# Row maxima of the next attention unit: spread over six pairs of key tiles instead of seven

## The chip, the core and the metric

The kernel runs on one core of a Trainium2 chip. The metric is the device time of one execution in microseconds (us); the figure for a kernel is the median of its runs. The engines are called as in the profile: PE (TensorE matrix products), PEld (TensorE loading its stationary operand), DVE (VectorE), ACT (ScalarE), POOL (GpSimd), SP (SyncE, which starts most DMAs here). Each engine works through its own queue in order.

## What is computed

One layer of a diffusion backbone on 2048 latent tokens and 256 context tokens, 1024 channels, in fp32: a modulated RMS norm, one wide input projection, two attention branches with gates, an output projection, a residual and a last norm. The branch the change touches is a full softmax attention of 8 heads, 2048 queries against 2304 keys (latent and context), key width 96, value width 64:

```python
sc = jnp.einsum('bqhd,bkhd->bhqk', qblk, k, preferred_element_type=jnp.float32) * scale
p = jax.nn.softmax(sc, axis=-1).astype(v.dtype)
return jnp.einsum('bhqk,bkhd->bqhd', p, v)
```

The other branch (neighbourhood attention on the 32 x 64 grid) runs at the same time in this kernel, as a side stream.

## The kernel before, in words

**Stages.** Projections first (up to about 1056 us of the profiled execution), then the attention stage (to about 2185 us), then the output projection. The change is in the attention stage.

**Units.** The full attention is cut into `nu = 32` units: unit `u` is head `u // 4` and a block of 512 queries `u % 4`. Within a unit the 2304 keys are 18 tiles of 128, taken in `NKP = 9` pairs (`kp` = 0 to 8). For each of the two tiles of a pair, PE makes scores `S` of 128 keys x 512 queries in three products (fp32 split in a high and a low part), and ACT takes the exponential into the pair's tile `P` (L1278). POOL adds the pairs' `P` into `za`, the softmax denominators (L1286, L1288, one instruction per pair). Every second pair, PE multiplies four tiles of `P` with the values into `oacc` (L1235).

**The row maximum.** The exponential needs the row's maximum beforehand. It is computed one unit ahead, by `max_tasks(u + 1)`: 20 parts, each one product `pm` of 128 queries x 512 keys (every fifth one 256 keys) on PE and one `reduce_max` on DVE (L825); then `fold`, a last small maximum on DVE (L828) followed on POOL by `spread` (L812), which lays the 512 maxima on diagonals in the tile `md`; and at last `row`, a product `pmf` of `md` with ones on PE and a copy by ACT into row 97 of the next unit's queries `qh` (L834). The 20 parts and the fold are a list of 21 tasks. `more` emits tasks of it three times per pair; `row` is emitted in the middle of the last pair (`kp == NKP - 1`), after the first tile's scores, and `zp` (the sum of the previous unit's denominators) with it.

**The side stream.** `feed` emits tasks of the neighbourhood attention at the same three places, by a count of its own: score products `ns`, products for its maxima `nm` and `nc` (evicted by DVE, L886 and L897), diagonals `nmd` on POOL (L812), their products `nf`, sums `nza` on POOL (L956, L937), values `no` on PE.

**What sets the order.** PE's order in this stage is the order in which the code emits its products (`keep_in_program_order`, L807-809). The queues of DVE, ACT, POOL and SP are put in order by a scheduler from the same code. All of `S`, `pm`, `pmf`, `zp`, `ns`, `nm`, `nc`, `nf` share five PSUM banks: `psm` gives them out from `psM` (three) and `psS` (two) in turn, and a bank is free again when DVE or ACT has read it. `P` has `PB = 8` tiles.

Of the kernel before, what the change touches and what calls it, by code (L numbers as in the profile page):

```python
# [64 lines left out]
def tile_hybrid_layer(ctx: ExitStack, tc: tile.TileContext, I: dict, out: bass.AP, dbg=None):  # L65
# [74 lines left out]
    def psm(name):  # L140
        if env["rot"] is not None:
            env["rot"] = (env["rot"] + 1) % 5
            if env["rot"] >= 3:
                return env["psS"].tile([P, W], F32, tag="S", name=name)
        return psM.tile([P, W], F32, tag="M", name=name)
# [627 lines left out]
    def load_qh(u):  # L773
        h, g = divmod(u, NB)
        qh = mq.tile([DK + 1, W], F32R, tag="qh", name=f"qh{u}", bufs=3)
        env["q"].dma_start(bc(qh[0:DK, :]), bc(qm[h][0, :, g * W:(g + 1) * W]))
        return qh

    def load_ql(u):
        h, g = divmod(u, NB)  # L780
        ql = mq.tile([DK, W], F32R, tag="ql", name=f"ql{u}")
        env["q"].dma_start(bc(ql), bc(qm[h][1, :, g * W:(g + 1) * W]))
        return ql

    def load_k(h):
        i = h % 2
        env["q"].dma_start(bc(Kh[i][0:NOPE, :]), bc(kmS[h][0]))
        env["q"].dma_start(bc(Kl[i][0:NOPE, :]), bc(kmS[h][1]))

    def load_v(h):  # L790
        vt = mv.tile([P, NKT, DV], F32, tag="V", name=f"V{h}")
        env["q"].dma_start(vt, vaS[:, h])
        return vt
# [12 lines left out]
    def mm(*args, **kw):  # L806
        ins = nc.tensor.matmul(*args, **kw)  # L807
        if pe["pin"]:
            tc.keep_in_program_order(ins)
# [5 lines left out]
    def max_tasks(u, qh):  # L815
        i = (u // NB) % 2
        m5 = mq.tile([P, 4, 5], F32, tag="m5", name=f"m5{u}")
        m1 = mq.tile([P, 4], F32, tag="m1", name=f"m1{u}")
        md = mq.tile([P, 4, P], F32R, tag="md", name=f"md{u}", bufs=1)

        def part(qt, ci):
            a, b = ci * W, min(NK, (ci + 1) * W)
            pm = psm(f"pm{u}_{qt}_{ci}")
            mm(pm[:, :b - a], qh[0:DK, qt * P:(qt + 1) * P], Kh[i][0:DK, a:b], start=True, stop=True)
            nc.vector.reduce_max(m5[:, qt, ci:ci + 1], pm[:, :b - a], axis=AX.X)  # L825

        def fold():
            nc.vector.tensor_reduce(m1, m5, axis=AX.X, op=ALU.max, negate=True)  # L828
            spread(md, m1)

        def row():
            pm = psm(f"pmf{u}")
            mm(pm, onesr, md.rearrange("p t f -> p (t f)"), start=True, stop=True)
            nc.scalar.activation(qh[DK:DK + 1, :], pm[DK:DK + 1, :], AF.Copy)  # L834
            for f in zdefer:
                f()
            zdefer.clear()

        return [lambda q=qt, c=ci: part(q, c) for qt in range(4) for ci in range(5)] + [fold], row
# [119 lines left out]
    def n_pv(d, pair, pts, last):  # L959
        h = d["h"]  # L960
        acc = d["acc"]
        vs = d["v"][:, :, (h % 2) * DV:(h % 2 + 1) * DV]
        lists = []
        for t, pt in zip(pair, pts):
            l = []
            if t[0] == "c":
                _, qc, ct = t
                half, bank = divmod(qc, 2)
                l.append((acc[half * DV:(half + 1) * DV, bank, :], vs[:, 16 + ct, :], pt, ct == 0))
            else:  # L970
                _, rb, cb = t
                (r0, r1), (c0, c1) = TROW[rb], CREG[cb]
                ncl = c1 - c0
                for sg in range(4):
                    a, b = max(r0, sg * 8), min(r1, sg * 8 + 8)
                    if a >= b:
                        continue
                    half, bank = divmod(sg, 2)
                    o_ = acc[half * DV:(half + 1) * DV, bank, :].rearrange("p (r c) -> p r c", c=GW)
                    l.append((o_[:, a - sg * 8:b - sg * 8, c0:c1], vs[:, rb * 4 + cb, :],  # L980
                              pt[:, (a - r0) * ncl:(b - r0) * ncl].rearrange("p (r c) -> p r c", c=ncl), False))
            lists.append(l)
        if len(lists[0]) == 3:
            lists[1] = lists[1][::-1]
        n = max(map(len, lists))
        for k in range(n):
            for l in lists:
                if k < len(l):
                    o_, v_, p_, st_ = l[k]
                    mm(o_, v_, p_, start=st_, stop=last and k == n - 1, skip_group_check=True)  # L990
# [171 lines left out]
    with tc.high_priority(offset=HOIST):  # L1162
        tasks, row = max_tasks(0, qhs[0])
# [7 lines left out]
    def feed(target):  # L1171
        while fed[0] < target:
            w_ = next(stream, None)
            if w_ is None:
                fed[0] = 1e9
                return
            fed[0] += w_
# [43 lines left out]
    NKP = NKT // 2  # L1221
# [7 lines left out]
    def pv(u, kp, pt, acc, za, vt):  # L1229
        late.append((kp, pt))  # L1230
        if kp % PVB == PVB - 1 or kp == NKP - 1:
            env["burst"] = True
            for k, p_ in late:
                for x in range(2):
                    mm(acc[x * DV:(x + 1) * DV, :], vt[:, 2 * k + x, :], p_[:, x, :],  # L1235
                                     start=(k == 0), stop=(k == NKP - 1), skip_group_check=True)
            late.clear()
        if kp < NKP - 1:
            return None
        oraw = mo.tile([DV, W], F32, tag="or", name=f"or{u}")  # L1240
        nc.scalar.activation(oraw, acc[DV:P, :], AF.Copy)
        nc.vector.tensor_tensor(oraw, acc[0:DV, :], oraw, op=ALU.add)
        return finish_tasks(u, za, oraw, pt)

    pe["pin"] = True
    for u in range(nu):
        h, g = divmod(u, NB)
        i = h % 2
        qh, ql = qhs[u], qls[u]
        vt = Vt  # L1250
        tasks, row = [], None
        if u + 2 < nu:
            qhs.append(load_qh(u + 2))
        if u + 1 < nu:
            tasks, row = max_tasks(u + 1, qhs[u + 1])
        if g == NB - 1 and h + 1 < H:
            Vt = load_v(h + 1)
        acc = psO.tile([P, W], F32, tag="O", name=f"oacc{u}")
        za = mo.tile([P, 2, W], F32, tag="za", name=f"za{u}")
        done = 0  # L1260
        prev = None
        for kp in range(NKP):
            pt = mp.tile([P, 2, W], F32, tag="P", name=f"P{u}_{kp}", bufs=PB)
            def more(frac):
                nonlocal done
                want = min(len(tasks), int(len(tasks) * (kp + frac) / (NKP - 2.0) + 1))
                while done < want:
                    tasks[done]()
                    done += 1

            for x in range(2):
                ks = slice((2 * kp + x) * P, (2 * kp + x + 1) * P)
                sp = psm(f"S{u}_{kp}_{x}")
                n = 0
                for a, b, e in ((Kh[i], qh, DK + 1), (Kh[i], ql, DK), (Kl[i], qh, DK)):
                    mm(sp, a[0:e, ks], b[0:e, :], start=(n == 0), stop=(n == 2))
                    n += 1
                nc.scalar.activation(pt[:, x, :], sp, AF.Exp)  # L1278
                more(0.33 * x)
                if x == 0 and kp == NKP - 1 and row is not None:  # L1280
                    row()
                if x == 0:
                    feed(total_weight * (step + 0.5 - LEAD) / (nsteps - TAIL - LEAD))
            ve = nc.vector if kp in ZDVE.get(nu - u, ()) else nc.gpsimd
            if kp == 1:
                ve.tensor_tensor(za, prev, pt, op=ALU.add)  # L1286
            elif 1 < kp < NKP - (u + 1 == nu):
                ve.tensor_tensor(za, za, pt, op=ALU.add)  # L1288
            prev = pt
            if kp == 1 and u + 1 < nu:  # L1290
                qls.append(load_ql(u + 1))
            if g == 0 and kp == 1 and h + 1 < H:
                load_k(h + 1)
            if pend is not None:
                ftasks = pv(*pend) or ftasks
                if env.pop("burst", False):
                    while held:
                        n_pv(*held.pop(0))
            pend = (u, kp, pt, acc, za, vt)
            if kp >= 2 and ftasks:  # L1300
                ftasks.pop(0)()
            more(0.66)
            step += 1
            feed(total_weight * (step - LEAD) / (nsteps - TAIL - LEAD))
# [239 lines left out]
```

## Time and profile before

| | us |
|---|---|
| median of 3 runs | 2565.34 (2562.31 to 2571.34) |
| profiled execution | 2569.03 |
| its span in the trace | 2567.2 |
| PE busy in the span | 2505.7 (98%) |
| DVE, POOL, ACT busy | 1102.7, 1092.2, 905.3 |

The profiled execution is one more run; its span is the stretch in which the trace shows instructions, 1.8 us less than its time. PE is the busiest engine by far, so the time is read from where PE waits and from the clock that it was granted; the other engines matter where PE waits for them.

### The profile page before, as it was taken

The page shows a single profiled execution, that of the slowest core. Times are in us where ns is not written, and L with a number is a line of the kernel's source. Part 1 is how long each engine was busy: PE and PEld are TensorE (multiplying, and loading weights), DVE is VectorE, ACT ScalarE, POOL GpSimd, SP SyncE. Part 2 cuts the span into 40 slices and gives each one's busy share as a digit, 9 for nine tenths or more (in the row PEclk, how much of TensorE's full clock was granted, in tenths as well). Part 3 has the DMA queues.
Part 4 walks back from the last instruction along what each step waited for, and adds up shares of the span by engine and source line. Part 5 has one row for each costly group of instructions (what it writes and reads, how often), then busy time and mean ns, then how long its engine had stood idle before and what let it go on. Part 6 is the DMA issues. An engine that isn't in the chain of part 4 may idle for free.

```text
span 2567.2 us, 34839 instructions
## 1 busy us (share of the span) xinstructions
PE 2505.7 (98%) x12796; PEld 1839.1 (72%) x12796; DVE 1102.7 (43%) x2285; ACT 905.3 (35%) x1774; POOL 1092.2 (43%) x861
## 2 busy tenths in 40 slices
PE   7999999999999999999999999999999999999998
PEld 4878888877789888656555656665656664888998
DVE  4653222222311211355455635554646446455654
ACT  3664432222222122234444434444444444212221
POOL 1312111111310000368787868777887885132220
PEclk9999999999999999999999989999999999999999
DMA  7535765456553465712324141514140334765542
GB/s 263 191 92 164 257 222 185 140 167 191 178 159 109 122 214 194 184 48 68 80 51 107 46 101 36 121 39 109 39 110 26 81 106 144 246 190 161 181 148 70
DMA packets 182979, 342.86 MB, mean 134 GB/s; under 512 B 25130, under 2 KB 95950, under 8 KB 175438
## 3 DMA queue, kind: packets, MB, share of 16 engines
q1 hardware_dynamic: 168872, 299.01, 38.9%
q0 software_dynamic: 13504, 41.35, 5.6%
q8 instruction: 100, 1.64, 0.3%
q14 instruction: 71, 0.58, 0.1%
q10 hardware_dynamic: 432, 0.28, 0.0%
HBM read 214.42 MB, written 126.13 MB: 133 GB/s over the span
## 4 chain that ended last, share of the span: by engine, by line
PE 88%; DVE 3%; DMA 3%; POOL 2%; issue 2%; ACT 1%; SPq 1%; POOLq 0%; ACTq 0%; DVEq 0%
PE accm L135 25%; PE S L807 15%; PE oacc L807 10%; PE pm L807 6%; PE f L135 5%; PE ya L135 4%; PE vacc L135 4%; PE nacc L226 3%; PE no L807 3%; PE accf L135 2%; PE accx L135 1%; PE qa_False L135 1%; PE pstl L185 1%; PE nm L807 1%; POOL za L1288 1%
## 5 line engine op out<-in xcount | busy, mean ns | idle before, releaser
L825 DVE TENSOR_REDUCE m<-pm 128x1 f32<-128x512 f32 (+1 forms) x640 | 387.6, 632 | 420.0 <-PE pm L807 414.3
L1288 POOL TENSOR_TENSOR za<-za,P 128x1024 f32<-128x1024 f32 x217 | 516.1, 2378 | 114.2 <-ACT P L1278 110.7
L1278 ACT ACTIVATE P<-S 128x512 f32<-128x512 f32 x576 | 342.9, 597 | 481.3 <-PE S L807 465.9
L135 PE MATMUL accm<-hh,whi 128*128 128x512 f32 x928 | 366.7, 395 | 0.0
L135 PE MATMUL accm<-hh,wlo 128*128 128x512 f32 x928 | 366.4, 395 | 0.0
L135 PE MATMUL accm<-hl,whi 128*128 128x512 f32 x928 | 366.3, 395 | 0.0
L807 PE MATMUL oacc<-P,V 128*64 128x512 f32 x1152 | 292.0, 624 | 0.0
L807 PE MATMUL S<-qh,Kh 97*128 97x512 f32 x576 | 240.4, 417 | 7.9 <-DVE m L825 4.3
L807 PE MATMUL S<-ql,Kh 96*128 96x512 f32 x576 | 230.7, 400 | 0.0
L807 PE MATMUL S<-qh,Kl 96*128 96x512 f32 x576 | 229.3, 398 | 0.0
L807 PE MATMUL pm<-Kh,qh 96*128 96x512 f32 (+1 forms) x640 | 222.6, 395 | 4.5 <-DVE m L825 3.3
L135 PEld LDWEIGHTS accm<-hh,whi 128*128 128x128 f32 x928 | 174.1, 188 | 42.8 <-issue 0.8
L135 PEld LDWEIGHTS accm<-hh,wlo 128*128 128x128 f32 x928 | 174.1, 188 | 42.5
L135 PEld LDWEIGHTS accm<-hl,whi 128*128 128x128 f32 x928 | 174.1, 188 | 41.6
L807 PEld LDWEIGHTS pm<-Kh,qh 96*128 96x128 f32 x640 | 121.1, 189 | 106.7 <-issue 62.5
L135 PE MATMUL ya<-u,woh 128*128 128x256 f32 x1024 | 185.0, 283 | 2.0 <-DVE t L1346 2.0
L807 PEld LDWEIGHTS oacc<-P,V 128*64 128x64 f32 x1152 | 70.4, 139 | 137.6 <-issue 137.3
L135 PE MATMUL f<-wfh,y 128*128 128x512 f32 (+1 forms) x528 | 162.2, 387 | 6.2 <-DMA wfh<-wfS 4.0
L135 PEld LDWEIGHTS ya<-u,woh 128*128 128x128 f32 x1024 | 160.1, 192 | 3.2 <-DVE t L1346 2.4
L807 PEld LDWEIGHTS S<-qh,Kh 97*128 97x128 f32 x576 | 109.9, 191 | 54.0 <-issue 12.4
L135 PE MATMUL ya<-u,wol 128*128 128x256 f32 x512 | 144.8, 283 | 0.0
L356 ACT ACTIVATE g<-accm 128x512 f32<-128x512 f32 x88 | 52.2, 593 | 248.8 <-PE accm L135 202.6
(1928 smaller groups left out, 4253.2 us busy)
## 6 DMA issues: line engine op xcount, KB each, us to landing
rawc<-in_wch SPq DMA_DIRECT2D x30, 512.0 KB
KA<-kB SPq DMA_DIRECT2D x16, 576.0 KB
xl<-in_xb SPq DMA_DIRECT2D x32, 256.0 KB
wm<-in_wmodb SPq DMA_DIRECT2D x8, 1024.0 KB
kmS<-sk POOLq DMA_DIRECT2D x32, 256.0 KB, 3.8
qR<-q SPq DMA_DIRECT2D x16, 512.0 KB
qm<-sq POOLq DMA_DIRECT2D x32, 256.0 KB, 4.1
woS<-ps SPq DMA_DIRECT2D x16, 512.0 KB
```

Of the source, the lines that this page charges most:

```text
L135: nc.tensor.matmul(acc, a, b, start=(i == 0), stop=(i == n - 1))
L185: nc.tensor.matmul(pst[32 * j:32 * j + 32, :w], ones[:, 0:32], sq[:, :w], start=(kt < 4), stop=(kt >= 4))
L226: nc.tensor.matmul(acc[:, :n], a[:, k, sl], b[:, k, :n], start=(k == 0 and q == 0), stop=(k == KT - 1 and q == 2))
L356: nc.scalar.activation(s1, acc, AF.Sigmoid)
L807: ins = nc.tensor.matmul(*args, **kw)
L825: nc.vector.reduce_max(m5[:, qt, ci:ci + 1], pm[:, :b - a], axis=AX.X)
L1278: nc.scalar.activation(pt[:, x, :], sp, AF.Exp)
L1288: ve.tensor_tensor(za, za, pt, op=ALU.add)
```

## The change

One number: the divisor that spreads the 21 tasks over the unit.

```diff
             def more(frac):
                 nonlocal done
-                want = min(len(tasks), int(len(tasks) * (kp + frac) / (NKP - 2.0) + 1))
+                want = min(len(tasks), int(len(tasks) * (kp + frac) / (NKP - 3.0) + 1))
                 while done < want:
                     tasks[done]()
                     done += 1
```

Tasks emitted at the three places of a pair (after the first tile's scores, after the second's, at the pair's end), counted out from that line:

| pair | before | now |
|---|---|---|
| 0 | 1, 0, 1 | 1, 1, 1 |
| 1 | 2, 0, 1 | 1, 1, 1 |
| 2 | 2, 0, 1 | 2, 1, 1 |
| 3 | 2, 0, 1 | 1, 1, 1 |
| 4 | 2, 0, 1 | 2, 1, 1 |
| 5 | 2, 0, 1 | 1, 1, 1 |
| 6 | 2, 0, 1 | 1 (the fold) |
| 7 | 1 (the fold) | none |
| 8 | none | none |

`row` stays in pair 8, so two pairs lie between fold and row where there was one. No instruction is added or removed on any engine.

On PE, in pair 5 of unit 11 (`pm12_a_b` is the product of query block a and key block b for unit 12; `S11_5_x` the scores of tile x; `ns2` a score of the side stream). Before:

```order
L807 MATMUL S11_5_0_12004<-qh11_11198,Kh0_8342 128x512
L807 MATMUL S11_5_0_12004<-ql11_11555,Kh0_8342 128x512
L807 MATMUL S11_5_0_12004<-qh11_11198,Kl0_8344 128x512
L807 MATMUL pm12_2_4_12009<-Kh1_8343,qh12_11493 128x256
L807 MATMUL pm12_3_0_12012<-Kh1_8343,qh12_11493 128x512
L807 MATMUL ns2_('w', 1, 3)_12015<-QQ_8341,KA_8339 128x360
L807 MATMUL ns2_('w', 1, 3)_12015<-QLt_8338,KBt_8340 128x360
L807 MATMUL S11_5_1_12022<-qh11_11198,Kh0_8342 128x512
L807 MATMUL S11_5_1_12022<-ql11_11555,Kh0_8342 128x512
L807 MATMUL S11_5_1_12022<-qh11_11198,Kl0_8344 128x512
L807 MATMUL pm12_3_1_12028<-Kh1_8343,qh12_11493 128x512
```

Now:

```order
L807 MATMUL S11_5_0_12013<-qh11_11198,Kh0_8342 128x512
L807 MATMUL S11_5_0_12013<-ql11_11558,Kh0_8342 128x512
L807 MATMUL S11_5_0_12013<-qh11_11198,Kl0_8344 128x512
L807 MATMUL pm12_3_2_12018<-Kh1_8343,qh12_11493 128x512
L807 MATMUL ns2_('w', 1, 3)_12021<-QQ_8341,KA_8339 128x360
L807 MATMUL ns2_('w', 1, 3)_12021<-QLt_8338,KBt_8340 128x360
L807 MATMUL S11_5_1_12028<-qh11_11198,Kh0_8342 128x512
L807 MATMUL S11_5_1_12028<-ql11_11558,Kh0_8342 128x512
L807 MATMUL S11_5_1_12028<-qh11_11198,Kl0_8344 128x512
L807 MATMUL pm12_3_3_12033<-Kh1_8343,qh12_11493 128x512
L807 MATMUL pm12_3_4_12037<-Kh1_8343,qh12_11493 128x256
```

Two products, then one, have become one, then two, and the last product of the unit (3_4) stands here instead of in pair 6.

On POOL, around the spread `md12` in the same unit (`P11_k` is pair k's tile). Before:

```order
L1288 TENSOR_TENSOR za11_11816<-za11_11816,P11_5_12003 128x1024
L956 TENSOR_TENSOR nza2_11145<-nza2_11145,np2_('w', 1, 3)_12016 128x15x24
L956 TENSOR_TENSOR nza2_11145<-nza2_11145,np2_('w', 2, 3)_12032 128x15x24
L1288 TENSOR_TENSOR za11_11816<-za11_11816,P11_6_12038 128x1024
L812 TENSOR_TENSOR md12_11812<-ident_63,m112_11811 128x512
```

Now:

```order
L1288 TENSOR_TENSOR za11_11816<-za11_11816,P11_5_12012 128x1024
L956 TENSOR_TENSOR nza2_11145<-nza2_11145,np2_('w', 1, 3)_12022 128x15x24
L812 TENSOR_TENSOR md12_11812<-ident_63,m112_11811 128x512
L956 TENSOR_TENSOR nza2_11145<-nza2_11145,np2_('w', 2, 3)_12041 128x15x24
L1288 TENSOR_TENSOR za11_11816<-za11_11816,P11_6_12047 128x1024
```

The spread has moved ahead of pair 6's addition; so it has in 30 of the 31 units that have one, and in the last of them (unit 30) it stays behind it.

On DVE, in unit 12, around the first window maxima of the side stream's next head (`nm4_0`, `nm4_1`; `nc4_0` its context maximum; L886 ISA with 128x1 reads the result out). Before:

```order
L825 TENSOR_REDUCE m513_12134<-pm13_3_1_12330 128x1
L897 TENSOR_REDUCE nmx4_12265<-nc4_0_12333 128x2
L825 TENSOR_REDUCE m513_12134<-pm13_3_2_12343 128x1
L825 TENSOR_REDUCE m513_12134<-pm13_3_3_12346 128x1
L886 ISA njk4_0_12288,nmx4_12265<-nm4_0_12286,bn4_11902 128x264
L886 ISA nmx4_12265 128x1
L886 ISA njk4_1_12305,nmx4_12265<-nm4_1_12303,bn4_11902 128x352
```

Now:

```order
L825 TENSOR_REDUCE m513_12134<-pm13_3_4_12339 128x1
L828 TENSOR_REDUCE m113_12135<-m513_12134 128x4
L897 TENSOR_REDUCE nmx4_12271<-nc4_0_12342 128x2
L886 ISA njk4_0_12294,nmx4_12271<-nm4_0_12292,bn4_11905 128x264
L886 ISA nmx4_12271 128x1
L886 ISA njk4_1_12314,nmx4_12271<-nm4_1_12312,bn4_11905 128x352
```

The two window maxima still stand behind row maxima whose products PE makes later; they now follow the context maximum of pair 5 directly instead of two row maxima of pair 6.

## Rows read from the trace of the kernel before

**Rows 1.** The page: busy time by engine; the chain that ended last, by engine.
```profile
PE 2505.7 (98%) x12796; PEld 1839.1 (72%) x12796; DVE 1102.7 (43%) x2285; ACT 905.3 (35%) x1774; POOL 1092.2 (43%) x861
PE 88%; DVE 3%; DMA 3%; POOL 2%; issue 2%; ACT 1%; SPq 1%; POOLq 0%; ACTq 0%; DVEq 0%
```

**Rows 2.** Windows: start:end, length, PE PEld DVE ACT POOL busy (instructions), PEclk, DMA.
```profile
1080.00:2185.00 1105.00, 1077.44 (x5207) 654.85 (x5207) 593.26 (x1187) 486.62 (x877) 848.24 (x506) 0.98 0.31 78
```

**Rows 3.** Waits, 1080 to 2185: who waited for whom, total, times, longest.
```profile
PEld pmf L807 <- POOL md L812: 16.8, 13, 3.5
PE pmf L807 <- POOL md L812: 11.8, 6, 3.0
```

**Rows 4.** Timeline of PE, four of the six waits for the spread: start, length, instruction.
```profile
1338.49 0.51 PE L807 MATMUL pmf<-md,onesr 128*128 128x512 f32 x1 [2.09 <-POOL md L812]
...
1482.44 0.49 PE L807 MATMUL pmf<-md,onesr 128*128 128x512 f32 x1 [2.23 <-POOL md L812]
...
1989.73 0.50 PE L807 MATMUL pmf<-md,onesr 128*128 128x512 f32 x1 [2.21 <-POOL md L812]
...
2157.71 0.79 PE L807 MATMUL pmf<-md,onesr 128*128 128x512 f32 x1 [3.05 <-POOL md L812]
```

**Rows 5.** Timeline of POOL ahead of the wait at 1482.44 (unit 11).
```profile
1474.76 2.38 POOL L1288 TENSOR_TENSOR za<-za,P 128x1024 f32<-128x1024 f32 x1
1477.08 0.96 POOL L956 TENSOR_TENSOR nza<-nza,np_('w', 1, 3)_12016 128x360 f32<-128x360 f32 x1
1478.12 0.95 POOL L956 TENSOR_TENSOR nza<-nza,np_('w', 2, 3)_12032 128x360 f32<-128x360 f32 x1
1479.03 2.36 POOL L1288 TENSOR_TENSOR za<-za,P 128x1024 f32<-128x1024 f32 x1
1481.35 1.04 POOL L812 TENSOR_TENSOR md<-ident,m 128x512 fp32r<-128x512 f32 x1
```

**Rows 6.** Timeline of DVE in pairs 5 to 7 of unit 11.
```profile
1472.91 0.69 DVE L825 TENSOR_REDUCE m<-pm 128x1 f32<-128x512 f32 x1
1473.52 0.52 DVE L953 TENSOR_TENSOR np_('w', 2, 3)_12032<-ns_('w', 2, 3)_12031,bt 128x360 f32<-128x360 f32 x1
...
1478.15 0.42 DVE L825 TENSOR_REDUCE m<-pm 128x1 f32<-128x256 f32 x1 [2.69 <-PE pm L807]
1478.61 0.17 DVE L828 TENSOR_REDUCE m<-m 128x4 f32<-128x20 f32 x1
```

**Rows 7.** Windows of 8 us behind the waits at 1338.49 and 1989.73.
```profile
1338.50:1346.50 8.00, 8.00 (x42) 4.32 (x43) 1.33 (x3) 2.39 (x6) 8.00 (x5) 0.79 0.52 130
...
1989.70:1997.70 8.00, 7.97 (x57) 5.01 (x59) 1.66 (x3) 2.87 (x6) 7.84 (x5) 1.00 0.15 49
```

**Rows 8.** DVE's fold and POOL's spread of unit 30, from the timelines.
```profile
2156.37 0.17 DVE L828 TENSOR_REDUCE m<-m 128x4 f32<-128x20 f32 x1
2156.62 1.04 POOL L812 TENSOR_TENSOR md<-ident,m 128x512 fp32r<-128x512 f32 x1 [1.35 <-DVE m L828]
```

**Rows 9.** Unit 12: PE's product nm4_0 and a wait, DVE's maximum of nm4_0, a window.
```profile
1504.45 0.29 PE L807 MATMUL nm<-NKm,NQs 112*128 112x264 f32 x1
...
1513.46 0.80 PE L807 MATMUL nc<-NKm,NQs 112*128 112x256 f32 x2 [0.78 <-DVE m L825]
1517.72 0.42 DVE L886 CUSTOM_DVE_ANT_1 njk<-nm,bn 128x264 f32<-128x264 f32 x1
1509.00:1526.00 17.00, 14.45 (x36) 7.54 (x37) 5.61 (x14) 3.68 (x7) 6.52 (x4) 0.60 0.00 0
```

**Rows 10.** Groups by form, 1080 to 2185: DVE's full row maxima, busy, mean ns, idle before.
```profile
L825 DVE TENSOR_REDUCE m<-pm 128x1 f32<-128x512 f32 x485 | 322.8, 686 | 295.7 <-PE pm L807 291.1
```

**Rows 11.** Tile pm, 1080 to 2185: who waited for these products and maxima, us, times.
```profile
  PEld S L807: 7.9, 12
...
  PE S L807: 3.0, 5
  PE pm L807: 2.6, 2
```

## The prediction

> **What bounds the kernel now.** I read the page first: PE is busy for 98% of the span and holds 88% of the chain that ended last [rows 1], so nothing but PE's waits and PE's clock can give time back. Then the window over the attention stage: of 1105 us PE is busy for 1077, its mean granted clock is 0.98, and DVE and POOL work 54% and 77% of the stage [rows 2]. So 28 us are idle there, and a clock of 0.98 means another 22 us or so lost at the half rate. The list of waits then says who holds PE: the largest single cause is the product `pmf`, which waits for POOL's spread `md`, 11.8 us in six waits [rows 3]. The rest is many small waits for PSUM banks. The change acts on exactly these two kinds, and only in this stage.
>
> Four of the six waits are shown [rows 4], 9.6 us together; the two left out, in units 18 and 29, share the other 2.2 us. Five of the six have one cause, and one another. In unit 11 the maxima are folded by 1478.8 [rows 6], yet the spread starts at 1481.35 [rows 5]: POOL is behind, and the addition of pair 6 (2.36 us) stands ahead of the spread in its queue. PE is ready for `pmf` 2.23 us before it gets it [rows 4], at 1480.2. In unit 30 it is the other way round: POOL sat idle for 1.35 us until DVE folded at 2156.37 [rows 8]; there DVE is late.
>
> **The change part by part.** No instruction is added or taken away; what changes is places in queues.
>
> *1. The spread moves ahead of pair 6's addition on POOL.* For unit 11 I lay the new order on the old times: pair 5's addition and the first `nza` sum end at 1478.04, the spread runs to 1479.1 (1.04 us) [rows 5], and PE asks for it at 1480.2: 1.1 us to spare. The fold must be there by 1478.04. The last product now stands where the product of DVE's row at 1472.91 stood, with one short product and one side-stream row behind it; adding 0.42, 0.52 and 0.17 to the end of that row (1473.60) gives about 1474.7 [rows 6], 3 us early. At the other four waits of this kind the spread passes at least one addition of 2.36 us too, and the longest of the five waits is 2.23 us [rows 4, 5]; so I take all five as gone: 11.8 - 3.05 = 8.8 us, with 8.8 us as the best and half of it as the worst (if the fold or another piece of POOL's backlog is late in its place). What the spread passes is late by its 1.04 us: the addition of pair 6 and, in some units, an `nza` sum or an `nmd`. Behind these additions stand the reuse of a `P` tile (eight tiles, so eight pairs of cover), the unit's last sum, which PE asks for in the next unit's pair 8, and the side stream's `nf`. If that cover were gone, 1.04 us per unit would show, at most where POOL is behind, five times: 5 us; I take nothing.
>
> *2. The clock behind these waits.* Behind the wait at 1338.49 the clock reads 0.79 over 8 us, which is 8 x 0.21 = 1.7 us lost, and so it does, three times in all, behind the waits of units 11 and 18; behind the one at 1989.73 it reads 1.00 [rows 7]. The clock is either 1.2 or 2.4 GHz, and it fell after idle stretches of about 2 us in three cases of four. Waits gone, I take 3 x 1.7 = 5.1 us back; between 0 and 5.1 us.
>
> *3. Unit 30.* The spread stays behind pair 6's addition, and the fold is set by DVE, which is busy with the output stage's first inputs there. The products come a pair earlier but DVE's queue ahead of the fold holds nearly the same work. I take 0, between 0 and -3.05 us.
>
> *4. More row maxima per pair.* Pairs 0, 2 and 4 get one product more, pair 6 loses three. In pairs 2 and 4 the extra one stands right ahead of the four value tiles, when PE needs no new bank for a while; but the odd pairs now end on two products and the next pair begins with two, so four maxima (4 x 0.69 us [rows 10]) fall due around one group of scores, where it was three. That happens about twice in a unit, in 31 units: 62 places. The nearest rows are the waits for DVE's maxima as they are: 3.0 + 2.6 us on PE in seven waits, and 7.9 us on PEld, which mostly hide behind running products [rows 11]. Taken in proportion to the density (20 products in 6 pairs instead of 6 1/3) hardly 1 us is added; if all the PEld waits came to the surface, 7.9 us. I take +2 us, near the low end, because DVE has 295.7 us of idle time ahead of these maxima [rows 10]; the range is 0 to +7.9 us, and rival B is beyond it.
>
> *5. The banks held by the side stream.* In unit 12 PE makes `nm4_0` at 1504.45, but DVE reads it only at 1517.72, since its queue has row maxima of later products ahead [rows 9], as the order on DVE in the section on the change shows. Two of five banks are held meanwhile, PE stumbles in short waits, and the clock over 1509 to 1526 reads 0.60: 17 x 0.40 = 6.8 us lost, and 17 - 14.45 = 2.55 us idle [rows 9]. Now DVE reads it after the context maximum of pair 5, so between `nm4_1` and its release PE makes seven groups instead of ten. Three tenths of 6.8 + 2.55 = 9.4 us is -2.8 us; in unit 16 the next head's first maximum is held somewhat longer than before, for which I set +0.8 us. I take -2 us; the bounds are -9.4 us (the whole episode goes) and +9.4 us (a second one like it).
>
> The sum: -8.8 - 5.1 + 0 + 2 - 2 = **-13.9 us**. Against the profiled execution's own 2569.0 us that is 2555.1 us; the median of the runs is 3.7 us lower than that execution, so the forecast for the median is 2565.3 - 13.9 = 2551.4 us, **2551 us**. The work in other stages is the same.
>
> **The rivals.**
>
> *A. The waits go, but not the time: about 2559 us.* Half of the waits stay in another form (the spread stands in time, but now waits for a fold that DVE delays, or PE meets POOL's backlog later at `nf`), so -4.4 us instead of -8.8 and half of the clock, -2.6; with parts 4 and 5 as taken, -7 us. For it speaks that POOL is 77% busy in the stage and its backlog is work, not order [rows 2]; against it that the fold is 3 us early in unit 11 by its rows [rows 6], and that nothing asks POOL for a result within the next pairs.
>
> *B. Denser maxima make PE stumble: slower, about 2575 us.* In unit 12, with banks short, a wait of 0.78 us for DVE and shorter ones like it stand in the long stretch at 0.60, worth 9.4 us [rows 9]. If four maxima around one group of scores are too many for five banks, such stretches come elsewhere too. The point from which it decides: without part 4's +2 and part 5's -2 the gain is 13.9 us, so two such episodes (18.8 us) bring the kernel back to about 2570 us, and slower by over 0.3% (7.7 us) needs 21.6 us, two and a bit; I price it at 2.5, 2565.3 - 13.9 + 23.5 = 2575 us. Speaking against it: in 28 or so of the other units with three maxima there is no such stretch, and the extra product mostly stands ahead of the value tiles. The Trainium skill (TensorE: Matmul & The Clock Gate, section "A second HAM failure mode: psum-queue depth-cycling") describes this: a kernel that cycles through PSUM banks leaves PE idle for so short and so often that the clock swings between its two levels; by that rule the change, which asks more of the banks, would end as B. The trace agrees with it at this one stretch and shows no other like it in the stage.
>
> *C. The unit 12 episode goes altogether: about 2544 us.* Then part 5 is -9.4 instead of -2: 2565.3 - 21.3 = 2544 us. Seven groups on three banks may be few enough; the order alone can't tell.
>
> *D. The change doesn't do what it says.* The order shows the spread moved in 30 of 31 units; only in unit 30 is it not, which is part 3. No chance of its own.
>
> **How the numbers follow.** Forecast (2546 to 2557 us) 0.45; C (2539 to 2546) 0.16; A (2557 to 2566) 0.26; B (2566 to 2585) 0.13. The range that holds the time 8 times in 10 leaves a tenth at each end: 2541 to 2569 us. A measurement of this kernel can tell about 0.3%, 7.7 us, from no change: faster means below 2557.6, slower above 2573.0. Faster: forecast and C, and a little of A, 0.61. Slower: most of B, 0.10. Within 0.3%: 0.29.
>
> **What would show it right or wrong.** Part 1 is right if the list of waits has `pmf` behind `md` at about 3 us, one wait, in unit 30; wrong if several of 1 to 2 us are left. Part 2: the windows behind pair 8 of units 7, 11 and 18 read 1.00. Part 3: the wait of unit 30 stays between 2 and 3 us. Part 4: who waited for the maxima: PE's share stays under 8 us; over 15 us it was mis-sized. Part 5: the stretch of unit 12 reads a mean clock over 0.60 and less idle time. B shows as a stretch of a clock of 0.60 or less in any other unit. The prediction as a whole is wrong if PE's idle time in the stage falls by 9 us and the span doesn't, or if the clock of the stage falls under 0.98.

## The result: 29 us faster, twice the forecast

The changed kernel takes 2535.8 us, the median of four runs (2531.7 to 2539.3), beside 2564.6 us for the kernel before (2562.3 to 2571.3): a ratio of 0.988, 95% interval 0.986 to 0.989. Measured once more beside other kernels it was 2535.6 us, a ratio of 0.988 (0.987 to 0.990). The forecast was 2551 us with a range from 2541 us on; the sign was right, the size was half of what came, and the time lies 5 us below the range. Its profiled execution took 2537.2 us, its span 2535.4 us.

The page answers [rows 1] with busy time by engine and the chain by engine:

```profile
PE 2489.2 (98%) x12796; PEld 1833.4 (72%) x12796; DVE 1105.9 (44%) x2285; ACT 903.1 (36%) x1774; POOL 1093.5 (43%) x861
PE 89%; DMA 3%; DVE 3%; SPq 1%; ACT 1%; issue 1%; POOL 1%; POOLq 0%; DVEq 0%; ACTq 0%
```

PE has the same 12796 instructions and is busy for 16.5 us less. It did no less work: the granted clock, averaged over the execution, has gone from 0.987 to 0.995, so fewer of its instructions ran at the half clock. The window over the same stretch of the attention stage answers [rows 2] (columns as there):

```profile
1080.00:2185.00 1105.00, 1088.84 (x5423) 675.36 (x5422) 604.82 (x1197) 486.33 (x885) 848.79 (x510) 0.99 0.33 85
```

216 PE instructions more fit into the same 1105 us, PE is idle for 16 us instead of 28, and the clock has gone from 0.98 to 0.99. Of the waits behind the spread, [rows 3], this is what is left:

```profile
PEld pmf L807 <- POOL md L812: 3.6, 1, 3.6
PE pmf L807 <- POOL md L812: 3.2, 1, 3.2
```

One wait, the one of unit 30. To see where the rest went, I cut the stage into its 32 units: a unit's time runs from the start of its first product `S<-qh,Kh` to the start of the next unit's first (each unit has 18; the last unit runs to the end of the stage's last product `oacc`). Changed kernel less kernel before, in the two profiled executions:

| units | part of the prediction | forecast, us | measured, us |
|---|---|---|---|
| 7, 11, 18, 25, 29 | 1 and 2 | -13.9 | -3.9 -4.1 -3.9 -2.4 -0.5 = -14.8 |
| 30, 31 | 3 | 0 | +0.4 +0.6 = +0.9 |
| 12, 16 | 5 | -2.8 +0.8 = -2 | -6.8 +0.3 = -6.5 |
| the other 22, without unit 0 | 4 | +2 | -1.7 |
| 0 | none | none | -5.8 |
| outside the stage | none | 0 | -4.0 |

They add up to -31.8 us, the difference of the two spans (2567.2 and 2535.4). The last row is no effect of the change: what lies outside the stage was 1.9 to 6.6 us shorter than in that one execution of the kernel before in every later profile, in kernels that change a single unit too. Without it the stage is 27.8 us shorter, near the 28.8 us between the medians.

**Parts 1 and 2, as forecast.** POOL in unit 11, which answers [rows 5], and PE's `pmf` there:

```profile
1461.95 2.38 POOL L1288 TENSOR_TENSOR za<-za,P 128x1024 f32<-128x1024 f32 x1
1464.29 0.96 POOL L956 TENSOR_TENSOR nza<-nza,np_('w', 1, 3)_12022 128x360 f32<-128x360 f32 x1
1465.21 1.04 POOL L812 TENSOR_TENSOR md<-ident,m 128x512 fp32r<-128x512 f32 x1
...
1467.13 2.39 POOL L1288 TENSOR_TENSOR za<-za,P 128x1024 f32<-128x1024 f32 x1
```
```profile
1467.48 0.40 PE L807 MATMUL pmf<-md,onesr 128*128 128x512 f32 x1
```

The spread ends at 1466.25, PE asks at 1467.48: 1.2 us to spare, where 1.1 us had been worked out from [rows 5]. The windows behind the `pmf` of units 7, 11 and 18, which answer [rows 7], read a full clock:

```profile
1328.80:1336.80 8.00, 8.00 (x52) 4.51 (x53) 2.87 (x5) 4.56 (x10) 8.00 (x7) 1.00 0.52 131
1467.50:1475.50 8.00, 8.00 (x57) 4.34 (x55) 1.38 (x2) 4.24 (x8) 7.76 (x4) 1.00 0.89 194
1714.60:1722.60 8.00, 8.00 (x57) 4.47 (x55) 1.30 (x2) 3.48 (x7) 7.76 (x6) 1.00 0.82 191
```

**Unit 0, which the prediction does not name.** In the kernel before, PE's waits in the first microseconds of the stage were these, with the two row maxima of DVE that released the first two:

```profile
1061.65 0.49 PE L807 MATMUL pm<-Kh,qh 96*128 96x512 f32 x1 [0.78 <-DVE m L825]
1062.93 0.50 PE L807 MATMUL S<-qh,Kh 97*128 97x512 f32 x1 [0.78 <-DVE m L825]
1064.53 0.79 PE L807 MATMUL S<-qh,Kh 97*128 97x512 f32 x1 [0.52 <-DVE m L825]
```
```profile
1060.90 0.69 DVE L825 TENSOR_REDUCE m<-pm 128x1 f32<-128x512 f32 x1 [0.25 <-PE pm L807]
1062.18 0.69 DVE L825 TENSOR_REDUCE m<-pm 128x1 f32<-128x512 f32 x1 [0.59 <-PE pm L807]
```

DVE reads at 1060.90 the product that PE has just made (it started at 1060.47), and is through at 1061.59; at 1061.65 PE starts the next one. It then waits for DVE to read that one (until 1062.87) before it starts a group of scores. So each waits for the bank of its immediate predecessor, although the stage has five banks. The whole unit, as a window of the kernel before and one of the changed kernel:

```profile
1057.80:1093.10 35.30, 33.08 (x127) 19.59 (x128) 19.25 (x45) 12.61 (x20) 21.19 (x12) 0.90 0.91 216
```
```profile
1055.60:1085.10 29.50, 29.36 (x127) 18.48 (x128) 19.19 (x45) 12.57 (x20) 21.09 (x12) 1.00 1.04 241
```

The same 127 PE instructions: 2.1 us less idle time, and 0.10 x 35.3 = 3.5 us less lost to the clock.

**Unit 12.** Windows over the unit, before and after, and the three waits that are left:

```profile
1489.10:1531.60 42.50, 39.56 (x151) 21.55 (x150) 18.50 (x36) 16.02 (x27) 23.28 (x13) 0.84 0.40 98
```
```profile
1472.50:1508.10 35.60, 33.55 (x151) 19.57 (x150) 18.77 (x36) 15.90 (x27) 26.43 (x15) 1.00 0.53 130
```
```profile
1493.08 0.50 PE L807 MATMUL pm<-Kh,qh 96*128 96x512 f32 x1 [0.75 <-ACT P L1278]
1495.77 0.39 PE L807 MATMUL pm<-Kh,qh 96*128 96x256 f32 x1 [0.79 <-DVE m L825]
1496.67 0.51 PE L807 MATMUL nc<-NKm,NQs 112*128 112x256 f32 x2 [0.52 <-DVE m L825]
```

Still 2.06 us of waits, where there were 2.94 us of idle time before; but the 0.16 x 42.5 = 6.8 us that the half clock took are gone.

**What the built program says.** Which of the five banks a tile gets is fixed when the kernel is built: the code asks the two pools for tiles in turn (three from the one, two from the other), but within a pool a tile gets whichever bank the scheduler takes for free at that point, and that can be the one just used. The banks in pairs 0 to 2 of unit 0, in PE's order:

```
before: S0_0_0 0  pm1_0_0 2  S0_0_1 1  pm1_0_1 3  S0_1_0 4  pm1_0_2 2  pm1_0_3 2  S0_1_1 2  pm1_0_4 3  S0_2_0 3
now:    S0_0_0 0  pm1_0_0 2  S0_0_1 1  pm1_0_1 3  pm1_0_2 4  S0_1_0 2  pm1_0_3 0  S0_1_1 1  pm1_0_4 3  pm1_1_0 4  S0_2_0 2
```

Bank 2 three times running and bank 3 twice: these are the three waits. Over the stage a tile gets the bank of the tile made just before it 8 times in the kernel before (units 0, 9, 12, 23) and 7 times in the changed one (units 9, 12, 16, 27). Unit 12 has three of the 8 and four of the 7, so the number of repeats alone does not tell what a unit loses. So the change moved the spread and, by the way, dealt out the banks anew: units 0 and 23 are clear of it, 16 and 27 now have one each.

### The profile page after: what moved, and what is told of

Its sections match the earlier page's. It is cut to its first block, busy times and chain, and to the rows that moved or that the text cites. A ratio compares the mean times of both kernels' runs of the same rounds, so it can differ in the third digit from the quotient of the medians.

```text
span 2535.4 us, 34849 instructions
## 1 busy us (share of the span) xinstructions
PE 2489.2 (98%) x12796; PEld 1833.4 (72%) x12796; DVE 1105.9 (44%) x2285; ACT 903.1 (36%) x1774; POOL 1093.5 (43%) x861
## 4 chain that ended last, share of the span: by engine, by line
PE 89%; DMA 3%; DVE 3%; SPq 1%; ACT 1%; issue 1%; POOL 1%; POOLq 0%; DVEq 0%; ACTq 0%
PE accm L135 26%; PE S L807 15%; PE oacc L807 10%; PE pm L807 6%; PE f L135 5%; PE ya L135 4%; PE vacc L135 4%; PE nacc L226 3%; PE no L807 3%; PE accf L135 2%; PE accx L135 1%; PE nm L807 1%; DMA rz<-rzS 1%; PE pstl L185 1%; PE qa_False L135 1%
## 5 line engine op out<-in xcount | busy, mean ns | idle before, releaser
L807 PE MATMUL oacc<-P,V 128*64 128x512 f32 x1152 | 286.7, 614 | 0.0
```

## The experiments

The theory after this result: the gain has three causes, (a) the spread's place in POOL's queue, (b) the bank given twice running in unit 0, (c) the side stream's held banks in unit 12, which leave three banks for everything else. Rivals: that the earlier products do it by themselves, that the stretches of half clock in units 0 and 12 come and go by chance, or that unit 12's stumbling follows from unit 11's wait. "Unit" times are differences to the kernel before, as in the table above, each from one profiled execution.

**One group of units at a time.** First the change in unit 0 alone:

```diff
-                want = min(len(tasks), int(len(tasks) * (kp + frac) / (NKP - 2.0) + 1))
+                want = min(len(tasks), int(len(tasks) * (kp + frac) / (NKP - (3.0 if u == 0 else 2.0)) + 1))
```

> The denser spread only in unit 0; the other units as in the kernel before. Theory (order in the unit): in the profile of before, unit 0 has three PE waits for banks (0.78, 0.78, 0.52 us) around 1063 us and then 6.8 us at the half clock, and in the changed kernel neither; if the order of the products in unit 0 did that, unit 0 takes about 29.5 us here instead of 35.3 us, and the kernel gains 5 to 6 us (ratio 0.998). Rival (chance of the execution): the half clock there comes and goes by itself; unit 0 may then read 35 us here, and the times are the same as before within 2 us. Rival (my prediction's sum): nothing in unit 0, 0 us.

2563.7 us beside 2567.3, ratio 0.998 (0.997 to 0.999). Unit 0 is 5.7 us shorter and at full clock; unit 12, built as before, reads 42.5 us and 0.84 again:

```profile
1055.90:1085.50 29.60, 29.41 (x127) 18.49 (x128) 19.20 (x45) 12.62 (x20) 21.14 (x12) 1.00 1.04 240
1483.30:1525.80 42.50, 39.56 (x152) 21.57 (x151) 18.50 (x36) 16.01 (x27) 23.29 (x13) 0.84 0.40 99
```

The gain of unit 0 belongs to what the edit does in that unit. Then the five units with a wait behind POOL, by the same line with `u in (7, 11, 18, 25, 29)`:

> The denser spread only in units 7, 11, 18, 25 and 29, where the product pmf waited for the spread behind POOL's addition. Theory: the pmf waits of these units go, and with them 14 to 15 us (2550 us, ratio 0.994); unit 12 keeps its long stretch at the half clock (42 us) and unit 0 its 35 us. Rival (unit 12's stretch is a follow-up of unit 11's wait 27 us earlier): unit 12 falls to about 36 us here too, and the kernel gains 21 us. Rival (the waits are worth only their own 8.8 us and the clock comes back as low elsewhere): 9 us.

2550.2 us beside 2567.3, ratio 0.993 (0.992 to 0.994). One `pmf` wait is left (unit 30), the five units are 14.8 us shorter, just as in the changed kernel. Unit 12 is 1.1 us shorter only: it does not follow from unit 11. Unit 0, unaltered, had a shorter stretch of half clock here (-1.4 us). Then unit 12 alone, `u == 12`:

> The denser spread only in unit 12. Theory (the banks held by nm4_0 and nm4_1 are free sooner by the order in this unit): unit 12 takes 35 to 36 us instead of 42.5, no half clock of 13.65 us there, and the kernel gains 7 us (ratio 0.997). Rival (follow-up of unit 11's wait, which stays here): unit 12 stays at 42 us, 0 us. Rival (my prediction's part 5): about three tenths, 2.8 us, with a shorter stretch at the half clock left.

2562.1 us beside 2567.3, ratio 0.998 (0.997 to 0.999); unit 12 is 5.2 us shorter, while unit 11 keeps its wait:

```profile
1487.20:1524.40 37.20, 35.16 (x150) 20.06 (x150) 18.78 (x36) 15.90 (x27) 23.18 (x13) 0.95 0.42 105
```

A clock of 0.95, 1.9 us lost, where the first profile of the changed kernel had 1.00. Which of the two comes differs from execution to execution: the second profile of the changed kernel, below, has 0.95 too.

**The fold left where it was.** Products as in the changed kernel, but the fold emitted in pair 7:

```diff
-                want = min(len(tasks), int(len(tasks) * (kp + frac) / (NKP - 2.0) + 1))
+                want = min(len(tasks) - (kp < NKP - 2), int(len(tasks) * (kp + frac) / (NKP - 3.0) + 1))
```

> The products spread over six pairs in all units as in the changed kernel, but the fold left in pair 7. Theory (the waits for the spread come from the place of the fold and the spread in POOL's queue): the pmf waits of units 7, 11, 18, 25, 29 are back, about 9 us, and the half clock behind some of them, so the gain against before is only what units 0 and 12 give, 12 to 13 us, and some 15 us are lost against the changed kernel (about 2551 us). Rival (the products' earlier end alone does it, since POOL then has less backlog): the pmf waits stay away and the time is that of the changed kernel, 2536 us.

My expectation fell: 2538.6 us beside 2567.3, ratio 0.989 (0.988 to 0.990), the changed kernel's time, and the five units 14.8 us shorter. But the rival's reason is not shown by it either, for POOL's row in unit 11 reads

```profile
1460.40 0.97 POOL L956 TENSOR_TENSOR nza<-nza,np_('w', 1, 3)_12022 128x360 f32<-128x360 f32 x1
1461.33 1.04 POOL L812 TENSOR_TENSOR md<-ident,m 128x512 fp32r<-128x512 f32 x1
1462.33 0.97 POOL L956 TENSOR_TENSOR nza<-nza,np_('w', 2, 3)_12041 128x360 f32<-128x360 f32 x1
```

Though the code emits the fold in pair 7, the scheduler puts the spread ahead of pair 6's addition in 28 of the 30 units (not in units 0 and 26, where PE does not wait for it either). So it is the earlier end of the products that moves the spread, not the place of the fold in the code; how the scheduler weighs this is not shown. To move the spread alone, it has to be pinned. This experiment does so, with the products as in the kernel before:

```diff
-            spread(md, m1)
+            ins = spread(md, m1)
+            if pe["pin"]:
+                tc.keep_in_program_order(ins)
...
-                ve.tensor_tensor(za, za, pt, op=ALU.add)
+                if kp != 6 or u > 29:
+                    ve.tensor_tensor(za, za, pt, op=ALU.add)
...
             more(0.66)
+            if kp == 6 and u < 30:
+                more(0.67)
+                tc.keep_in_program_order(ve.tensor_tensor(za, za, pt, op=ALU.add))
```

> Only POOL's order is changed: the products and maxima stay spread over seven pairs, as in the kernel before, and the spread md is put ahead of pair 6's addition on POOL in units 0 to 29; PE, DVE and ACT have the order of before. Theory (the waits are a matter of POOL's order alone): pmf waits only in unit 30, units 7, 11, 18, 25 and 29 are shorter by 14 to 15 us in sum as in the changed kernel, units 0 and 12 keep their 35.3 and 42.5 us, the time is about 2552 us (ratio 0.994). Rival (the earlier end of the products is needed, because the spread now waits for the fold in POOL's queue and holds up the additions): waits of about 1 us stay at pmf and the gain is under 7 us.

2549.2 us beside 2566.3, ratio 0.993 (0.992 to 0.995). The five units are 14.6 us shorter, units 0 and 12 unchanged (-0.1 and 0.0 us). POOL in unit 11, and PE:

```profile
1472.70 0.96 POOL L958 TENSOR_TENSOR nza<-nza,np_('w', 2, 3)_12032 128x360 f32<-128x360 f32 x1
1473.62 1.04 POOL L812 TENSOR_TENSOR md<-ident,m 128x512 fp32r<-128x512 f32 x1
1474.62 2.38 POOL L1308 TENSOR_TENSOR za<-za,P 128x1024 f32<-128x1024 f32 x1
```
```profile
1474.71 0.50 PE L807 MATMUL pmf<-md,onesr 128*128 128x512 f32 x1
```

Just in time. Parts 1 and 2 are a matter of POOL's order; no product has to move. The opposite, the products of the changed kernel with the spread pinned behind pair 6's addition (the fold emitted in pair 7, `keep_in_program_order` on the spread and on pair 6's addition):

> The opposite: products and maxima over six pairs as in the changed kernel, but the spread md is held behind pair 6's addition on POOL in units 0 to 29. Theory (POOL's order): the pmf waits of about 2 us in units 7, 11, 18 and 25 come back with their half clock; against the changed kernel 12 to 15 us are lost, and what is left against before is units 0 and 12, about 12.6 us (ratio 0.995). Rival (with the products done earlier the fold is early and POOL's backlog is another): the waits stay away and the time is that of the changed kernel, ratio 0.988.

2573.4 us beside 2566.3, ratio 1.003 (1.002 to 1.004): slower than the kernel before, and 38 us slower than the changed kernel, more than twice what I expected.

```profile
PE pmf L807 <- POOL md L812: 20.7, 14, 3.8
```

In seven units (2, 6, 7, 10, 14, 18, 27) an `nza` sum stands between addition and spread as well, and the spread starts 0.8 to 4.5 us later in its unit than in the kernel before. Unit 27 alone lost 7.2 us; there the addition itself stood behind a sum for which POOL sat idle:

```profile
2060.51 1.01 POOL L958 TENSOR_TENSOR nza<-nza,np_('w', 0, 2)_16997 128x384 f32<-128x384 f32 x1 [2.06 <-ACT np_('w', 0, 2)_16997 L956]
```

Where only the addition stands ahead, as in unit 11, the wait is 2.0 us and the unit as long as before (-0.2 us). In units 8 and 15 the spread stayed ahead of the addition, and they take as long as in the changed kernel. So the direction is as the theory has it; the size is more than a restoration, because the pins moved more of POOL's queue than the spread.

**One step denser.** The same line with `NKP - 4.0`:

> One step further: the same products over five pairs (divisor NKP - 4). Theory (the gain from POOL's order is complete with six pairs, and density costs nothing there): what is left to gain is the wait in unit 30, 3 us, and the density now begins to cost: waits of PE for DVE's maxima of the 0.5 to 0.8 us kind in several units, each with some us at the half clock, so 0 to +10 us against the changed kernel (2536 to 2546 us). Rival (the earlier the better): 2530 us or less. Rival B of the prediction (dense maxima make PE stumble), only one step later: 2555 us or more.

2540.5 us, ratio 0.990 (0.989 to 0.992), beside 0.988 for the changed kernel measured with it: about 5 us given back, within what the theory expected. Waits of PE for row maxima, from who waited for the products `pm` in the changed kernel and, in the second fence, over five pairs (us, times):

```profile
  PE pm L807: 1.8, 3
  PE S L807: 1.5, 2
```
```profile
  PE S L807: 3.4, 6
  PE pm L807: 1.3, 1
```

The half clock that the expectation added to these waits did not come: in both kernels the clock from 1058 to 2155 us reads 1.00, and PE is idle for 18.8 us at five pairs (second line) where it is 16.0 us in the changed kernel's profile beside it:

```profile
1058.00:2155.00 1097.00, 1081.04 (x5279) 660.32 (x5281) 606.65 (x1206) 489.13 (x886) 860.28 (x511) 1.00 0.33 84
1058.00:2155.00 1097.00, 1078.25 (x5251) 657.80 (x5249) 598.12 (x1202) 485.54 (x878) 857.89 (x508) 1.00 0.33 83
```

So five pairs cost about 5 us. Whether density does it is not shown, for POOL's order and the banks are other ones here too. The changed kernel once more:

> The changed kernel once more, beside the others on this chip: ratio 0.988 again, units 0 and 12 at 29.5 and 35.6 us again if their gain is one of the order; if it was chance of the execution, one of them reads 35 or 42 us.

Unit 0 was 5.7 us shorter again, unit 12 5.3 us (37.2 us, clock 0.95):

```profile
1471.20:1508.40 37.20, 35.15 (x155) 20.07 (x152) 18.79 (x36) 15.96 (x27) 26.50 (x15) 0.95 0.51 124
```

**The banks alone.** In unit 0 of the kernel before only the turn of the two pools is shifted; every engine's order is row for row that of before, and no tile in unit 0 gets the bank of one of the two tiles before it:

```diff
+        if u == 0:
+            env['rot'] += 4
+        elif u == 1:
+            env['rot'] -= 4
```

> The order on PE, DVE, ACT and POOL is that of the kernel before, row for row; only the turn in which products get their PSUM banks is shifted by four places in unit 0. In the kernel before, three products or score groups in pairs 1 and 2 of unit 0 are built into the bank of the product made just before them, so that PE has to wait until DVE has read it. Theory (bank given twice running): the three waits of 0.78, 0.78 and 0.52 us and the half clock behind them go, unit 0 takes 29.5 us instead of 35.3, 5 to 6 us of gain (ratio 0.998), nothing else moves. Rival (density or order of the maxima in pairs 0 to 2 did it in the changed kernel): unit 0 stays at 35 us, 0 us.

2562.8 us beside 2568.1, ratio 0.998 (0.9965 to 0.9995); unit 0 is 5.6 us shorter, and its window reads

```profile
1052.10:1081.80 29.70, 29.33 (x127) 18.37 (x128) 19.14 (x45) 12.58 (x20) 21.15 (x12) 1.00 1.04 242
```

That settles unit 0: not the density, not the order, but the bank given twice. For unit 12, DVE's reading of the side stream's maxima is pinned to the order of the code, which puts it seven and six places ahead in DVE's queue (not eight and nine, as the expectation counted); the products stay as before:

```diff
-            nc.vector.reduce_max(m5[:, qt, ci:ci + 1], pm[:, :b - a], axis=AX.X)
+            ins = nc.vector.reduce_max(m5[:, qt, ci:ci + 1], pm[:, :b - a], axis=AX.X)
+            if pe["dve"]:
+                tc.keep_in_program_order(ins)
...
+        pe["dve"] = u in (12,)
```

(and the same two lines behind the window maximum, L886.)

> The products stand as in the kernel before; in unit 12 alone DVE reads the side stream's window maxima nm4_0 and nm4_1 in the order in which the code emits them, eight and nine places earlier in its queue, so that their two banks come free right away. Theory (held banks leave three, of which the next products get the same one twice running): most of the waits around 1509 to 1519 us go and the 13.65 us at the half clock with them, unit 12 takes 35 to 36 us instead of 42.5, about 6 us of gain (ratio 0.9975). Rival (DVE then waits for the bias tile and holds up the row maxima): unit 12 is not shorter, or longer.

2558.8 us beside 2568.1, ratio 0.997 (0.995 to 0.998). DVE reads `nm4_0` 1.2 us after PE starts it, instead of the 13.3 us of [rows 9], and unit 12 takes 34.5 us, 8.0 less, with one wait of 0.75 us left:

```profile
1505.95 0.28 PE L807 MATMUL nm<-NKm,NQs 112*128 112x264 f32 x1
...
1510.85 0.62 PE L807 MATMUL pm<-Kh,qh 96*128 96x256 f32 x2 [0.75 <-ACT P L1283]
```
```profile
1507.12 0.42 DVE L888 CUSTOM_DVE_ANT_1 njk<-nm,bn 128x264 f32<-128x264 f32 x1
```
```profile
1490.50:1525.00 34.50, 33.66 (x151) 19.39 (x151) 18.11 (x36) 16.02 (x27) 22.98 (x13) 1.00 0.49 123
```

The earlier reading frees the two banks, and in the built program it also leaves one of the unit's three repeats of a bank (the wait of 0.75 us stands at it). How much of the 8.0 us goes to the held banks and how much to the bank given twice is not shown apart; cause (c) is the two together.

**All three causes without the change.** The edits of the pinned spread, of the bank turn in unit 0 and of DVE's order in unit 12, put together on the kernel before, with its divisor `NKP - 2.0`:

> All products and maxima stay spread over seven pairs; the three causes alone are taken away: the spread md ahead of pair 6's addition on POOL in units 0 to 29, the bank turn shifted by four in unit 0, DVE's early reading of nm4_0 and nm4_1 in unit 12. Theory (these three are the whole gain of the change): 27 to 29 us, 2537 to 2539 us, ratio 0.989, as the changed kernel. Rival (the earlier products give something of their own): 2545 us or more.

2536.1 us beside 2568.1, ratio 0.988 (0.987 to 0.990): the whole gain of the change, with PE's order row for row that of the kernel before. Unit 0 -5.6, the five units -14.7, unit 12 -8.4 us. Unit 12 thus gains more than by the change itself (5.3 to 6.8 us): the sum agrees, not every piece.

**Both together.** The changed kernel with DVE's order pinned in units 9, 12 and 16 and the bank turn shifted by one in units 12, 16 and 27; no tile then gets the bank of the tile just before it:

```diff
+        pe["dve"] = u in (9, 12, 16)
+        if u in (12, 16, 27):
+            env['rot'] += 1
+        elif u in (13, 17, 28):
+            env['rot'] -= 1
```

> The changed kernel, and DVE's reading of the side stream's window maxima in code order in units 9, 12 and 16, and the bank turn shifted by one in units 12, 16 and 27, so that no product is built into the bank of the product made just before it. Theory: the changed kernel's waits of 0.4 to 0.8 us in units 9, 12, 16 and 27 go, 4 to 5 us in sum with the half clock behind two of them, 2531 to 2533 us (ratio to the changed kernel 0.998). Rival (these waits are hidden elsewhere): 2536 us.

2529.8 us beside 2568.1, ratio 0.986 (0.984 to 0.987), the fastest of all and some 6 us ahead of the changed kernel's 2535.6 us, a little more than expected; the two stood beside the kernel before on separate occasions, so this difference is known to some 4 us. In the profiles units 9, 12, 16 and 27 are 7.5 us shorter in sum than in the changed kernel. In unit 12 no wait of PE is left:

```profile
1468.00:1501.00 33.00, 32.95 (x150) 19.62 (x150) 18.35 (x36) 15.91 (x27) 25.36 (x15) 1.00 0.57 138
```

## Why the prediction was half right

*Parts 1 and 2 (-13.9 us): right.* -14.8 us in the same five units, by the mechanism named, with the lead in unit 11 off by 0.1 us; the pinned spread (-14.6 us) shows it to be POOL's order. It holds unit by unit too: the waits of units 7, 11 and 18 with 1.7 us each come to 3.8, 3.9 and 3.7 us, where 3.9, 4.1 and 3.9 us went. The share of the clock is that of the one execution before from which it was read; others differ, as the last section shows. Rival A came about in small only. What the spread passed is late for PE at `nf`, which waits in units 19 and 26 of the changed kernel and did not before (units 15 and 23 with the spread pinned, which are 0.9 and 0.5 us longer):

```profile
1736.52 0.51 PE L807 MATMUL nf<-nmd,onesr 128*128 128x512 f32 x1 [1.04 <-POOL nmd L812]
```

Unit 19 is no longer for it, since a wait of 0.99 us for DVE went. The 1.04 us is the size that I had named and set at nothing. The prediction gives no reason for the spread's move; in the expectation for the fold left in pair 7 I took the fold's place in the list of tasks for it, and that run shows that it is the end of the products.

*Part 3 (0): right in sum.* The wait in unit 30 stayed, at 3.2 us. In the second profile of the same kernel it was 1.5 us, with unit 30 2.6 us shorter than before and unit 31 2.5 us longer, so in sum -0.1 us.

*Part 4 (+2 us): wrong in sign, small.* The maxima got denser and PE's waits for them shorter ([rows 11]: 3.0 + 2.6 us, now 1.5 + 1.8 us), and the units in question are 1.7 us shorter, among them unit 27, longer by 1.0 us at a new repeat of a bank. So the sign is that of density and of the new deal of banks together. PEld's waits stayed as they were in sum: the 7.9 us before `S` have become 4.7, but those before `pm`, which [rows 11] leaves out, have grown from 3.6 us (first line) to 7.1:

```profile
  PEld pm L807: 3.6, 3
  PEld pm L807: 7.1, 8
```

At five pairs about 5 us are lost, for a cause that is open. Rival B did not come about, not even there. The rule that it drew on, in the Trainium skill (TensorE: Matmul & The Clock Gate, "A second HAM failure mode: psum-queue depth-cycling"), does describe units 0 and 12 of the kernel before, and their rows agree with it: waits of 0.3 to 0.8 us on banks, and a clock of 0.90 and 0.84 over the unit. But it is not density that brings these about: with the density of before both went, by the bank turn and by DVE's order.

*Part 5 (-2 us): mis-sized, -6.5 us.* The step that failed is "three tenths of 6.8 + 2.55". The idle time in unit 12 did fall by three tenths, from 2.94 to 2.06 us; the loss to the clock fell by all of its 6.8 us in one execution and by about 5 us in the second one and in the kernel with unit 12 alone changed. Here the loss to the clock did not go in proportion to the waits ahead of it; that was nearest to rival C, at -9.4 us, and it deserved more than 0.16.

*Unit 0 (-5.8 us): missing from the sum.* The step that failed is the first view: the window began at 1080 us, while the stage's first unit began at 1057.8. Three waits, 2.1 us together, and the half clock behind them stood in the 22 us that were left out:

```profile
1058.00:1080.00 22.00, 19.82 (x69) 11.40 (x69) 10.51 (x21) 7.03 (x11) 11.65 (x6) 0.84 1.02 244
```

With them in view the bank would have been the question: [rows 9] already show such waits in unit 12, and I read them as "banks held", which holds for two of five banks there, and not as "the same bank twice", which the bare list of waits does not tell.

*A slip in a rival.* Rival A's -7 us make 2558 us, not 2559; nothing rests on it.

## What to carry to other kernels

Where PE waits in short pieces for a reader, look whether it waits for the reading of the product just before: then the bank may have been handed out twice running, and shifting the turn of the pools adds no instruction; in unit 0 it gave 5.6 us, as much as the change of order (5.7 us). The Trainium skill (Perfetto Trace Analysis, "Optimizing Tensor Performance", Matmuls) asks that independent groups rotate through different banks; here three repeats of a bank within 3 us cost 5.6 us. A wait on an engine that is behind can be a matter of that engine's queue alone, as POOL's was here: see what of its work could stand behind the awaited instruction, and pin it; then read the whole queue again, for pins move more than the one instruction (38 us the wrong way, in the opposite experiment). And begin the window at the stage's first instruction, not at a round number.

## What the hardware showed that was not expected

Waits of 2.0 to 2.2 us in all, in one piece (`pmf`) or in three (unit 0), were mostly followed by a stretch at the half clock, but its length differs between executions of the same code. The `pmf` of unit 7, built as before, waited 2.09 us in the profile of the kernel before, and the 8 us behind it read 0.79 [rows 7]. In two other kernels it waited 2.08 us, and the 8 us from its start read 0.58 (bank turn shifted in unit 0, first line) and 1.00 (unit 12 alone changed, second line):

```profile
1328.50:1336.50 8.00, 7.98 (x36) 3.93 (x37) 0.66 (x1) 1.96 (x4) 8.00 (x5) 0.58 0.35 98
1336.70:1344.70 8.00, 8.00 (x53) 4.68 (x55) 1.88 (x3) 3.59 (x8) 8.00 (x5) 1.00 0.52 132
```

Unit 7 was 1.4 us longer in the one and 1.7 us shorter in the other, so the price of a single wait at the clock is known to some 3 us only from one execution. On the other hand, the units that a kernel leaves alone and that have no such stretch come out the same to about 0.05 us from profile to profile, so that effects of half a microsecond can be read unit by unit, where a ratio's interval is 2 to 5 us to either side.
